# One encoder layer in fp32: the mixer as a pinned list schedule, and half of its gates stored in the place of x

## The chip, the cores and the metric

The kernel runs on one NeuronCore of a Trainium2 chip. The time is the device time of one execution in microseconds (us); the kernel before was timed three times. TensorE does the matmuls (PE, and PEld for its weight loads), VectorE (DVE) and ScalarE (ACT) the elementwise work, GpSimd (POOL) the decay tiles, SyncE (SP) issues the loads of weights.

## The reference, cut to what matters

One layer over 256 tokens of 1024 features, all in fp32: a half-step feed-forward network, a mixer of two branches, a second half-step network. The change touches the mixer alone.

```python
x = x + 1/2 * SwiGLU_1(RMSNorm(x))
h = RMSNorm(x);  u = h @ W_in
a = MLA(...)     # 16 heads: norms of q and k, rope, softmax(q k) v
m = BiSSD(...)   # 4 groups of 8 heads, conv of width 5 + SiLU, forward and backward scans
x = x + W_out( sigmoid(gA) * (a @ P_A) + sigmoid(gB) * (m @ P_B) )
x = x + 1/2 * SwiGLU_2(RMSNorm(x))
```

W_in holds, side by side, the latent columns of the attention, the columns of the SSD groups (z, x, B, C and the step sizes dt) and the two gates gA and gB. A scan over a chunk of 128 tokens is a product with a matrix of decays, exp(a[l] − a[s]), where a are cumulated logarithms:

```python
seg = a_cs[..., :, None] - a_cs[..., None, :]
decay = jnp.exp(jnp.where(tril, seg, -jnp.inf))
cb = jnp.einsum('bclgn,bcsgn->bcgls', cc, bc)
y_diag = jnp.einsum('bcgls,bcghls,bcsghp->bclghp', cb, decay, xdt)
```

## The kernel before

Weights and activations are each split into two reduced-precision pieces, hi and lo, and a product is the sum of three matmuls. `wload` (L131) loads 128x1024 weights (512 KB, SP's queue, tile raw), ACT copies them to whi (L113), DVE subtracts to get wlo (L116). `wstat` (L157) then issues three matmuls (L163, L164, L165) for each of 8 slices of 128 features: 24 matmuls for one piece, called a half below. Four buffers each hold raw, whi and wlo; four PSUM banks serve these products (ps_in, ps_half) and four (ps_g) all else. Activations stand in SBUF with features on partitions: x, and its scaled split xs.

The mixer runs in these steps.

- The first projection, three blocks into ps_in, gives the latent columns and dt. R is the norm row (L113, from ps_rows L230), by which DVE scales x into xr, split to xs (8 slices), and the first projection into cr, split to cqh, cql, ckh, ckl.
- The dt chain ends in ps_acs, the cumulated logarithms. ACT's queue writes them to DRAM as scr, from which the decay tiles are fetched.
- `in_group` (L562 on) makes ten halves for each SSD group: six with the convolution (ACT L582, then four DVE operations L119 on the tile xz), four plain ones for z, and one SiLU over all five xz tiles (L594).
- `ssd_group`: ps_cb (L709) is the matrix cb, ps_xT the transposed x. For each pair of heads POOL fetches a tile E of 128x768 from scr (L734) and adds the decays (L741, four operations per head), ACT takes Exp (L750), DVE multiplies by cb and sums (L116), PE makes ps_y (L760), DVE writes yg. A last step norms the group into ms. Six E buffers are shared by all heads.
- `attn_group`: eight groups of two heads, projection ps_qkv, transposes ps_qkT, scores ps_sc, softmax (L675), ps_pT, ps_o.
- `gates`: 16 halves through `half` (L792 on) into eight tiles gt; `branch0`: 8 halves of the SSD branch's output matrix for groups 0 and 1 into mpb. Sigmoids over gt follow (L837).
- The output: ps_ab (attention branch), ps_sb (second half of the SSD branch), the gated sum, and the last product ps_o, added to x.

The order of the steps is set by hand: `put` gives each step a number on a common line and `fill` spreads the halves of one group over one unit of it. All steps are written out in the order of these numbers, and a scheduler then orders each engine by its own rules, with the split of weights at a higher priority; the evictions of the last blocks (`paced`) hold back some Exps. The halves of group g+1 stand beside the scan of group g; the 16 gate halves stand beside the scan of group 3, after all blocks:

```python
        if g + 1 < G:
            xz, units = in_group(g + 1)
            if g == 2:
                units = units + [lambda c=c, j=j: branch0(c, j) for c in range(4) for j in range(2)]
        else:
            units = [lambda c=c, j=j: gates(c, j) for c in range(8) for j in range(2)]
        fill(g + F0, g + 1 + F0, units)
```

The functions that the change touches, with the line numbers of the profile:

Of the kernel before, what the change touches and what calls it, by code (L numbers as in the profile page):

```python
# [8 lines left out]
F32 = mybir.dt.float32  # L9
# [6 lines left out]
P = 128  # L16
# [21 lines left out]
PLC = ()  # L38
PLG = ()


A0 = -0.1293
DA = 0.2126
DB = 0.1251
S0 = 0.0991
DS = 0.1864
SF = 0.994

LA = 0.0317
LC = 0.0503  # L50
LF = 0.2546
HOLD = 0
AN = 1
F0 = 0.0148
F1 = -0.5421
# [7 lines left out]
G = 4  # L63
# [15 lines left out]
def _parts(value, bits, n):  # L79
    out = []  # L80
    rest = value
    for _ in range(n - 1):
        e = np.floor(np.log2(abs(rest)))
        q = 2.0 ** (e - bits + 1)
        part = np.floor(rest / q) * q
        out.append(float(part))
        rest -= part
    out.append(float(np.float32(rest)))
    return out


def build(ctx, tc, A, out, dbg=None):
# [87 lines left out]
    def rsqrt(y, v, n):  # L180
# [4 lines left out]
        ts(t, v.bitcast(I32), 1, None, ALU.logical_shift_right)  # L185
        ts(y.bitcast(I32), t, -1.0, float(0x5F3759DF), ALU.mult, ALU.add)
        ts(w, v, -0.5, None, ALU.mult)
        for _ in range(3):
            tt(a, y, y, ALU.mult)
            tt(a, a, w, ALU.mult)  # L190
            stt(y, a, 1.5, y, ALU.add, ALU.mult)
# [158 lines left out]
    scr = tc.dram_tile([32, 6, P], F32, name="scr")  # L350
    aneg = cp.tile([P, 64], F32, name="aneg")
# [69 lines left out]


    with ExitStack() as es:
# [30 lines left out]
        for k in range(KD):  # L454
            xr = m0.tile([P, T], F32, tag="xr", name="xr", bufs=2)
            stt(xr, x[:, k], vec[:, V_MIX + k:V_MIX + k + 1], R, ALU.mult, ALU.mult)
            split(xs[:, k, 0], xs[:, k, 1], xr)

        def latent(src, hi, lo, vcol, n):
            acc = sm.tile([P, T], F32, tag="nacc", name="lacc", bufs=1)  # L460
            for i, s in enumerate(src):
                if i == 0:
                    S.activation(acc, s, AF.Square)
                else:
                    sq = sm.tile([P, T], F32, tag="nsq", name="lsq", bufs=1)
                    S.activation(sq, s, AF.Square)
                    tt(acc, acc, sq, ALU.add)
                split(hi[:, i], lo[:, i], s, vec[:, vcol + i:vcol + i + 1])
            v = mp.tile([P, 2], F32, name=f"v_{vcol}", tag=f"v_{vcol}")
            ts(v, token_sums(ps_g, acc, "g"), 1.0 / n, EPS, ALU.mult, ALU.add)  # L470
            return v

        vq = latent(craw[0:3], cqh, cql, V_QA, 384.0)
        vk = latent(craw[3:5], ckh, ckl, V_KVA, 256.0)
        rk = mp.tile([P, 2], F32, name="rk")
        rsqrt(rk, vk, 2)
        hc = mp.tile([P, 2, 2], F32, name="hc")
        ts(hc[:, 0], vq, EPS * HD, None, ALU.mult)

        pt = gbank("ps_smt")  # L480
        for t in range(2):
            TE.transpose(pt[:, t * P:(t + 1) * P], craw[5][:, t * P:(t + 1) * P], ident)
        copy(smt, pt[:, :T].rearrange("p (a b) -> p a b", a=2))
        kpe = smt[:, :, 64:96]


        H = ROPE // 2
        kr = mp.tile([P, 2, ROPE], F32, name="kr")
        krs = m0.tile([P, 2, ROPE], F32, name="krs")
        kss = mp.tile([P, 2], F32, name="kss")  # L490
        tt(krs, kpe, kpe, ALU.mult)
        V.tensor_reduce(out=kss, in_=krs, axis=mybir.AxisListType.X, op=ALU.add)
        tt(kr, kpe, CCk, ALU.mult)
        tt(krs[:, :, 0:H], kpe[:, :, H:], SSk[:, :, 0:H], ALU.mult)
        tt(krs[:, :, H:], kpe[:, :, 0:H], SSk[:, :, H:], ALU.mult)
        tt(kr, kr, krs, ALU.add)
        ts(hc[:, 1], kss, EPS * HD, None, ALU.add)
# [3 lines left out]
        e = m0.tile([P, 2, 64], F32, name="dt_e")  # L501
        dt = m0.tile([P, 2, 64], F32, name="dt")
        tt(u, smt[:, :, 0:64], row[:, R_DTB:R_DTB + 64].unsqueeze(1).to_broadcast([P, 2, 64]), ALU.add)
        stt(e, u, -1.0, u, ALU.mult, ALU.max)
        S.activation(e, e, AF.Exp, scale=-1.0)
        S.activation(aneg, row[:, R_AL:R_AL + 64], AF.Exp)
        q = m0.tile([P, 2, 64], F32, name="dt_q")
        ts(q, e, 2.0, None, ALU.add)
        V.reciprocal(out=q, in_=q)
        tt(e, e, q, ALU.mult)  # L510
        tt(q, e, e, ALU.mult)
        pl = m0.tile([P, 2, 64], F32, name="dt_p")
        ts(pl, q, 1.0 / 17.0, None, ALU.mult)
        for c in (15.0, 13.0, 11.0, 9.0, 7.0, 5.0, 3.0):
            stt(pl, pl, 1.0 / c, q, ALU.add, ALU.mult)
        stt(pl, pl, 1.0, e, ALU.add, ALU.mult)
        ts(u, u, 0.0, None, ALU.max)
        stt(dt, pl, 2.0, u, ALU.mult, ALU.add)
        da = m0.tile([P, 2, 64], F32, name="da")
        stt(da, dt, -1.0, aneg.unsqueeze(1).to_broadcast([P, 2, 64]), ALU.mult, ALU.mult)  # L520
        dump("dt", dt)

        sgt = m0.tile([P, 2, P], F32, name="sgt")
        ts(sgt[:, 0], triF, 1.0, None, ALU.subtract)
        ts(sgt[:, 1], triB, 1.0, None, ALU.subtract)
        pa = gbank("ps_acs")
        for o, c, m in ((0, 0, sgt[:, 0]), (0, 1, triF), (32, 0, triB), (32, 1, sgt[:, 1])):
            TE.matmul(pa[:, c * 64 + o:c * 64 + o + 32], m, da[:, c, o:o + 32], start=True, stop=True)
        acs = m0.tile([P, 2, 64], F32, name="acs")
        V.tensor_copy(acs, pa[:, :P].rearrange("p (a b) -> p a b", a=2))  # L530
        nacs = mp.tile([P, 2, 64], F32, name="nacs")
        ts(nacs, acs, -1.0, None, ALU.mult)
        dup = m0.tile([P, 2, 2, 64], F32, name="dup")
        V.tensor_copy(dup, acs.unsqueeze(2).to_broadcast([P, 2, 2, 64]))
        pd = gbank("ps_dup")
        for c in range(2):
            TE.transpose(pd[:, c * P:(c + 1) * P], dup[:, c].rearrange("p a b -> p (a b)"), ident)
        acsT = m0.tile([P, T], F32, name="acsT")
        copy(acsT[0:64], pd[0:64, 0:T])
        for d in range(2):  # L540
            a = acsT[32 * d:32 * d + 32].rearrange("p (a b) -> p a b", a=2)
            o = 4 - 4 * d
            nc.scalar.dma_start(scr[:, o:o + 2], a)
            nc.scalar.dma_start(scr[:, 2 + d], a[:, 1 - d])

        lnd = mp.tile([P, 2, 64], F32, name="lnd")
        ts(u, dt, 2.0 ** -120, None, ALU.max)
        S.activation(lnd, u, AF.Ln)
        S.activation(e, lnd, AF.Exp, scale=-1.0)
        tt(e, e, u, ALU.mult)  # L550
        stt(lnd, e, -1.0, lnd, ALU.add, ALU.add)
        dump("acs", acs)
# [5 lines left out]
        m0_es.close()  # L558
        at_es = es.enter_context(ExitStack())
        at = at_es.enter_context(pool("attn", reuse_waits="tile"))  # L560

        paced = []

        def in_group(g):
            xz = [None] * 5
            cur = {}

            def half(c, j):  # L570
                if j == 0:
                    xz[c] = ss.tile([P, 2, T], F32, tag="xz", name="xz", bufs=10)
                    cur["ps"] = ps_mm.tile([P, 2, T], F32, tag="mm", name="ps_in1")
                xc, ps = xz[c], cur["ps"]
                (pc,) = wload(A["w_in1"][g, c, :, 1024 * j:1024 * j + 1024], [1024],
                              pool_lo=(0,) if 2 * c + j in PLC else ())
                wstat(ps[:, j], [(pc, 0, KD)], xs, 0, True, True)
                if c < 3:
                    i = 2 * c + j
                    ci = V_CW + (6 * g + i) * CW  # L580
                    cb = V_CB + 6 * g + i
                    last = S.activation(xc[:, j], ps[:, j], AF.Identity, bias=vec[:, cb:cb + 1],  # L582
                                        scale=vec[:, ci + 2:ci + 3])
                    for w in (0, 1, 3, 4):
                        s = w - 2
                        a0, a1 = max(0, -s), min(T, T - s)
                        stt(xc[:, j, a0:a1], ps[:, j, a0 + s:a1 + s], vec[:, ci + w:ci + w + 1],
                            xc[:, j, a0:a1], ALU.mult, ALU.add)
                elif j:
                    last = S.activation(xc, ps, AF.Copy)  # L590
                if c == 4 and j:
                    with tc.issue_after(last.ins), tc.high_priority():
                        for xc in xz:
                            last = S.activation(xc, xc, AF.Silu)  # L594
# [377 lines left out]
```

## Time and profile before

| | us |
|---|---|
| median of 3 runs | 808.74 |
| lowest and highest | 803.48, 808.98 |
| profiled execution | 806.14 |
| its span, first to last instruction | 804.2 |
| mixer, from R to the first ps_sb | 208.0 to 567.4 |
| first matmul of ps_cb, groups 0 to 3 | 271.4, 327.7, 403.9, 483.7 |
| gate halves on PE | 459.4 to 535.5 |
| decay tiles, first fetch to start of the last operation | 246.1 to 520.9 |

The page is made from one profiled execution. A row of instructions names line, engine, operation, output and inputs, shapes and count, then busy time and the mean of one in ns, then the idle time of the engine ahead of them and whose end released it. Matmuls are pipelined, so the mean of one is longer than the step from one to the next. The granted clock is the share of TensorE's full clock that was given.

### The profile page before, as it was taken

Reading aid. Unit: us, or ns where it says so; the run is one execution under the profiler, and the core shown is the slowest. Engines: PE = TensorE matmul, PEld = TensorE weight load, DVE = VectorE, ACT = ScalarE, POOL = GpSimd, SP = SyncE. Lnnn points to the kernel's source line nnn. Section 1 sums busy time; section 2 is a strip of 40 time slices with the busy share of each in tenths; the row PEclk is TensorE's granted clock in tenths of the full one; section 3 lists DMA queues with packets and bytes.
Section 4 is the critical chain, followed back from the end, with each engine's and each line's share of the span. In section 5 each row is a group of like instructions: output and inputs, shape, how many; then the busy total and the mean of one; then the engine's idle time right before and its main releaser. Section 6 shows DMA issues by size and latency. Waiting matters only on the chain.

```text
span 804.2 us, 13859 instructions
## 1 busy us (share of the span) xinstructions
PE 770.6 (96%) x5122; PEld 689.1 (86%) x5122; DVE 630.6 (78%) x1269; ACT 503.2 (63%) x887; POOL 169.1 (21%) x170
## 2 busy tenths in 40 slices
PE   7999999999989998899899989999999999999997
PEld 6888888888988887788888888898998888888886
DVE  5999887667788797899888877787787878877553
ACT  6666665555366787768679657767455666655441
POOL 0000000000004985855914482400000000000000
PEclk9999999999999999999999999999999999999999
DMA  7677764667117446247443744452655555554662
GB/s 270 198 229 236 224 230 142 182 189 221 51 57 232 152 163 226 76 146 243 125 146 122 241 150 138 143 184 88 210 174 185 182 185 188 188 194 129 204 206 72
DMA packets 43235, 139.10 MB, mean 173 GB/s; under 512 B 5152, under 2 KB 7200, under 8 KB 43168
## 3 DMA queue, kind: packets, MB, share of 16 engines
q1 hardware_dynamic: 40272, 125.43, 48.7%
q0 software_dynamic: 2560, 12.58, 4.9%
q8 instruction: 40, 0.66, 0.3%
q10 hardware_dynamic: 336, 0.20, 0.1%
q14 instruction: 27, 0.22, 0.1%
HBM read 137.05 MB, written 1.15 MB: 172 GB/s over the span
## 4 chain that ended last, share of the span: by engine, by line
PE 78%; DVE 13%; ACT 5%; issue 2%; DMA 1%; SPq 0%; DVEq 0%; ACTq 0%
PE ps_gu L176 20%; PE ps_d L176 10%; PE ps_gu L175 9%; PE ps_d L175 5%; DVE wlo L116 4%; PE ps_in L163 3%; PE ps_in L165 3%; PE ps_in L164 3%; PE ps_sc L666 2%; PE ps_y L760 2%; ACT whi L113 2%; PE ps_half L163 1%; PE ps_half L165 1%; PE ps_half L164 1%; DVE xz L119 1%
## 5 line engine op out<-in xcount | busy, mean ns | idle before, releaser
L113 ACT ACTIVATE whi<-raw 128x1024 fp32r<-128x1024 f32 (+4 forms) x260 | 250.9, 968 | 176.8 <-PE ps_d L176 51.5
L116 DVE TENSOR_TENSOR wlo<-raw,whi 128x1024 fp32r<-128x1024 f32 (+4 forms) x260 | 288.1, 1112 | 84.7 <-ACT whi L113 83.1
L176 PE MATMUL ps_gu<-xs,whi 128*128 128x512 f32 x704 | 243.0, 398 | 0.6 <-DVE xs L119 0.5
L175 PE MATMUL ps_gu<-xs,wlo 128*128 128x256 f32 x616 | 173.4, 281 | 3.6 <-DVE wlo L288 3.6
L741 POOL TENSOR_SCALAR E<-E,nacs 128x256 f32<-128x256 f32 (+1 forms) x128 | 148.8, 1178 | 25.7 <-DMA E<-scr 25.4
L176 PEld LDWEIGHTS ps_gu<-xs,whi 128*128 128x128 f32 x704 | 126.9, 189 | 25.3 <-DVE xs L119 1.2
L175 PEld LDWEIGHTS ps_gu<-xs,wlo 128*128 128x128 f32 x616 | 117.0, 190 | 8.3 <-DVE wlo L288 4.3
L176 PE MATMUL ps_d<-hs,whi 128*128 128x512 f32 x352 | 122.5, 393 | 0.0
L163 PE MATMUL ps_in<-xs,whi 128*128 128x256 f32 x368 | 109.1, 297 | 9.6 <-DVE xz L119 3.7
L165 PE MATMUL ps_in<-xs,wlo 128*128 128x256 f32 x368 | 107.4, 293 | 4.0 <-DVE wlo L116 4.0
L164 PE MATMUL ps_in<-xs,whi 128*128 128x256 f32 x368 | 107.1, 291 | 0.5 <-DVE xs L119 0.5
L175 PE MATMUL ps_d<-hs,wlo 128*128 128x256 f32 x336 | 94.7, 282 | 0.0
L734 POOL DMA_DIRECT2D E<-scr x32 | 18.0, 564 | 327.1 <-DVE wlo L116 245.7
L163 PEld LDWEIGHTS ps_in<-xs,whi 128*128 128x128 f32 x368 | 72.6, 198 | 13.4 <-ACT whi L113 5.0
L176 PEld LDWEIGHTS ps_d<-hs,whi 128*128 128x128 f32 x352 | 65.2, 188 | 13.8
L165 PEld LDWEIGHTS ps_in<-xs,wlo 128*128 128x128 f32 x368 | 72.5, 198 | 5.1 <-DVE wlo L116 4.6
L164 PEld LDWEIGHTS ps_in<-xs,whi 128*128 128x128 f32 x368 | 72.7, 198 | 1.7 <-issue 0.8
L175 PEld LDWEIGHTS ps_d<-hs,wlo 128*128 128x128 f32 x336 | 63.1, 188 | 0.7
L119 DVE SCALAR_TENSOR_TENSOR xz<-ps_in,vec,xz 128x254 f32<-128x254 f32 (+1 forms) x96 | 44.8, 477 | 6.0 <-ACT xz L582 5.5
L750 ACT ACTIVATE E<-E,lnd 128x256 f32<-128x256 f32 (+1 forms) x128 | 48.5, 450 | 0.0
L113 ACT ACTIVATE hs<-sg 128x256 fp32r<-128x256 f32 x44 | 18.1, 416 | 32.1 <-DVE sg L116 32.1
L163 PE MATMUL ps_half<-xs,whi 128*128 128x256 f32 x128 | 36.9, 289 | 0.0
(234 smaller groups left out, 1422.3 us busy)
## 6 DMA issues: line engine op xcount, KB each, us to landing
raw<-in_w_gu SPq DMA_DIRECT2D x86, 512.0 KB, 4.2
raw<-in_w_in SPq DMA_DIRECT2D x62, 512.0 KB, 4.7
raw<-in_w_d SPq DMA_DIRECT2D x32, 384.0 KB, 3.2
E<-scr POOLq DMA_DIRECT2D x32, 384.0 KB, 4.9
raw<-in_w_d SPq DMA_DIRECT2D x32, 320.0 KB, 3.4
raw<-in_w_sb SPq DMA_DIRECT2D x16, 512.0 KB, 4.2
raw<-in_w_ab SPq DMA_DIRECT2D x8, 512.0 KB, 3.8
raw<-in_w_o SPq DMA_DIRECT2D x8, 512.0 KB, 4.7
```

Source lines behind the costliest of these rows:

```text
L113: S.activation(dst, src, AF.Copy, scale=scale)
L116: V.tensor_tensor(out=dst, in0=a, in1=b, op=op)
L119: V.scalar_tensor_tensor(out=dst, in0=a, scalar=s, in1=b, op0=op0, op1=op1)
L163: TE.matmul(ps, pc.hi[:, w], xh, start=first and i == 0, stop=False)
L164: TE.matmul(ps, pc.hi[:, w], xl, start=False, stop=False)
L165: TE.matmul(ps, pc.lo[:, w], xh, start=False, stop=last and i == len(ks) - 1)
L175: TE.matmul(ps[:, 0], pc.lo[:, w], xs[:, k0 + i, 0], start=False, stop=False)
L176: TE.matmul(ps, pc.hi[:, w], xs[:, k0 + i], start=a, stop=b)
L666: TE.matmul(sc[:, t * T:(t + 1) * T], qk[:HD, t * P:(t + 1) * P], qk[:HD, T:2 * T], start=True, stop=True)
L734: nc.gpsimd.dma_start(E, scr[h].unsqueeze(0).to_broadcast([P, 6, P]))
L741: nc.gpsimd.tensor_scalar(out=E[:, a:a + n], in0=E[:, a:a + n], scalar1=nacs[:, c, w:w + 1], scalar2=0.0, op0=ALU.add, op1=ALU.min)
L750: ends[1] = S.activation(E[:, a:a + n], E[:, a:a + n], AF.Exp, bias=lnd[:, c, w:w + 1])
```

## The change

The mixer after the first projection is no longer written step by step. A class `Plan` collects steps, each of one engine (T, V, A, G for POOL, S for the loads): a cost from a small model (a fixed part and a part per element), a key, the steps on which it depends, and the rings of buffers from which it takes or to which it gives back. `Plan.run` then makes a list schedule: of each engine it takes the first step by key that can begin earliest, adds 1300 ns where ACT's function table changes, and adds a margin between engines. The steps are traced in that order, and each is pinned behind the step before it on its engine. Loads, splits, evictions, the operations of the norms and the parts of a scan are steps of their own; a half's 24 matmuls are three steps.

```diff
+class Plan:
+    FIX = {"V": 70, "A": 90, "G": 700}
+    PER = {"V": 1.04, "A": 0.83, "G": 2.4}
...
+    def run(self):
...
+            if s["table"] and s["table"] != table:
+                cost += 1300
+                table = s["table"]
...
+        for s in order:
+            bb = self.tc.nc.cur_bb.bb
+            n = len(bb.instructions)
+            with self.tc.issue_after(last[s["eng"]]) if s["eng"] in last else ExitStack():
+                s["fn"]()
+            last[s["eng"]] = bb.instructions[-1]
```

The keys count halves. Four gate halves are mixed among the ten of group 1 and four among the ten of group 2; the eight branch halves are mixed among those of group 3; the other eight gate halves come last. A group's scan begins when its SiLU is done, with one pair of heads for every 2.5 halves (3.5 in groups 2 and 3); attention group g has the key 8 + 6.5 g.

```diff
-A0 = -0.1293
-DA = 0.2126
...
+AK = 8.0
+AKD = 6.5
...
+SD = (2.5, 2.5, 3.5, 3.5)
...
+EA = 2
...
+NGT = (0, 4, 4, 0)
...
-        fill(g + F0, g + 1 + F0, units)
...
+            mix(ins[g], gts[o:n]) if g < G - 1 else mix(brs, ins[g], gts[o:n])
+            o = n
+        order += gts[o:]
```

The first eight gate halves are written into x itself, two of its eight feature tiles to each gate tile. x is spilled to DRAM by POOL's queue for that, twice (once after the first network, once as a step of the plan), and read back into four tiles xq, which the last product then uses.

```diff
+    spill = tc.dram_tile([P, KD, T], F32, name="spill")
...
+    nc.gpsimd.dma_start(spill, x)
...
+        spilled = do("G", 560, -30, lambda: nc.gpsimd.dma_start(spill, x), size=1 << 20)
...
-        gt = [None] * 8
+        gt = [x[:, 2 * c:2 * c + 2] for c in range(4)] + [None] * 4
...
+        for c in range(4):
+            xq.append(ss.tile([P, 2, T], F32, tag="xz", name="xq", bufs=10))
+            nc.gpsimd.dma_start(xq[c], spill[:, 2 * c:2 * c + 2])
...
-                tt(x[:, d], x[:, d], ps[:, j], ALU.add)
+                tt(x[:, d], xq[c][:, j], ps[:, j], ALU.add)
```

The fetch of a head now depends on the decays of the head two before it (EA = 2); the six small copies on POOL (L733, HOLD) are gone; the sigmoids depend on all scans, all attention groups and all gate halves.

```diff
-                    if g == 0 and p:
-                        nc.gpsimd.tensor_copy(E[:, 0, 0:1], xz[HOLD + p][:, 0, 0:1])
...
+                    d = do("G", 560, kh - LF, fetch, [rows_ready] + begun[-EA:][:1], take=["E"], size=393216)
```

Three places show what the order of the engines becomes. First DVE at the mixer's start, before: the four wlo of the first blocks of group 0 stand ahead of the norm (nv and rs_t are its first operations).

```order
L116 TENSOR_TENSOR wlo<-raw,whi 128x1024 x3
L119 SCALAR_TENSOR_TENSOR x<-ps_d,x 128x256
L123 TENSOR_SCALAR sgt<-cst 128x128
L119 SCALAR_TENSOR_TENSOR x<-ps_d,x 128x256
L123 TENSOR_SCALAR sgt<-cst 128x128
L116 TENSOR_TENSOR wlo<-raw,whi 128x1024
L119 SCALAR_TENSOR_TENSOR xs<-x,vec,xs 128x256
L116 TENSOR_TENSOR nacc<-nacc,nsq 128x256
L125 TENSOR_SCALAR nv<-ps_sum 128x2
```

The same engine after, where the first wlo of group 0 stands:

```order
L221 TENSOR_TENSOR cr<-ps_in_2225,R 128x512
L221 TENSOR_TENSOR xs<-xr,xs 128x256
L224 SCALAR_TENSOR_TENSOR cql<-cr,vec,cqh 128x256
L224 SCALAR_TENSOR_TENSOR ckl<-cr,vec,ckh 128x256
L230 TENSOR_SCALAR v_2306<-ps_sum 128x2
L224 SCALAR_TENSOR_TENSOR ckl<-cr,vec,ckh 128x256
L773 TENSOR_TENSOR wlo<-raw,whi 128x1024
L221 TENSOR_TENSOR dt_u<-smt,row 128x128
```

The first wlo moved from ahead of the norm to behind the third cr, all scaled slices and the splits of the latents.

Second ACT at the end of group 1's blocks, before: between the last plain eviction of xz and the SiLU nothing of the gates stands.

```order
L113 ACTIVATE whi<-raw 128x576
L675 ACTIVATE pr,sme<-ps_sc,mx,hr 128x256 x2
L113 ACTIVATE whi<-raw 128x512
L590 ACTIVATE xz<-ps_in_3452 128x512
L594 ACT_TABLE_LOAD
L594 ACTIVATE xz<-xz 128x512 x5
```

The same engine after, at the same place (x<-ps_half is the eviction of a gate half into x's place):

```order
L218 ACTIVATE whi<-raw 128x576
L1110 ACTIVATE ysq<-yg 128x512 x2
L218 ACTIVATE xs<-ps_o 128x256
L218 ACTIVATE whi<-raw 128x512
L218 ACTIVATE x<-ps_half 128x256
L218 ACTIVATE whi<-raw 128x1024
L218 ACTIVATE xz<-ps_in_3638 128x512
L1194 ACT_TABLE_LOAD
L1194 ACTIVATE xz<-xz 128x512 x5
```

A gate half, with its whi, its matmuls and its eviction, now stands among the blocks, four times in each of groups 1 and 2.

Third POOL in the last group's scan, before: fetches of one or two tiles at changing distances.

```order
L741 TENSOR_SCALAR E<-E,nacs 128x256
L734 DMA E<-scr 128x768
L741 TENSOR_SCALAR E<-E,nacs 128x256
L741 TENSOR_SCALAR E<-E,nacs 128x128 x2
L741 TENSOR_SCALAR E<-E,nacs 128x256
L734 DMA E<-scr 128x768 x2
```

The same engine after, one pair of heads and the fetches of the next:

```order
L1052 DMA E<-scr 128x768 x2
L1057 TENSOR_SCALAR E<-E,nacs 128x256
L1057 TENSOR_SCALAR E<-E,nacs 128x128 x2
L1057 TENSOR_SCALAR E<-E,nacs 128x256 x2
L1057 TENSOR_SCALAR E<-E,nacs 128x128 x2
L1057 TENSOR_SCALAR E<-E,nacs 128x256
L1052 DMA E<-scr 128x768 x2
```

Each pair's two fetches now stand directly ahead of the eight decay operations that use them, behind those of the pair before.

More of the change, by code (lines that the diff above doesn't have):

```diff
@@ L538, in build @@
[L538 to L549, printed above, removed]
@@ L556, in build @@
         mpb = mp.tile([P, 8, T], F32, name="mpb")
-        m0_es.close()
-        at_es = es.enter_context(ExitStack())
[L560 to L570, printed above, removed]
-                if j == 0:
-                    xz[c] = ss.tile([P, 2, T], F32, tag="xz", name="xz", bufs=10)
[L573 to L594, printed above, removed]
-                if c < 3 or j:
-                    paced.append(last)
-            return xz, [lambda c=c, j=j: half(c, j) for c in range(5) for j in range(2)]
```

848 lines of the change are left out of this document (581 added, 267 removed).

## The prediction

> **What bounds the kernel now.** I read the page first (busy times of the engines), then the mixer cut into stretches, then the waits inside them, last the single rows at its start. The page's first part:
>
> ```profile
> PE 770.6 (96%) x5122; PEld 689.1 (86%) x5122; DVE 630.6 (78%) x1269; ACT 503.2 (63%) x887; POOL 169.1 (21%) x170
> ```
>
> TensorE is busy 770.6 of 804.2 us, so less than 34 us can be won by order alone. The next view is the busy time by stretch: from the mixer's norm row R at 208 us to the first matmul of each SSD group (ps_cb at 271.4, 327.7, 403.9, 483.7) and on to the first ps_sb. Columns: the stretch, its length, PE, PEld, DVE, ACT and POOL busy with counts, granted clock, DMA share, GB/s. The last line is the first three stretches in one.
>
> ```profile
> core 0: us, PE busy (x) PEld busy (x) DVE busy (x) ACT busy (x) POOL busy (x), PEclk, DMA share, GB/s
> 208.00:271.40 63.40, 58.19 (x453) 55.90 (x454) 51.82 (x145) 41.22 (x75) 18.04 (x22) 0.97 0.40 127
> 271.40:327.70 56.30, 50.71 (x363) 43.85 (x362) 47.16 (x116) 41.25 (x86) 42.62 (x44) 0.97 0.50 165
> 327.70:403.90 76.20, 67.96 (x499) 62.08 (x498) 69.96 (x172) 57.00 (x116) 56.16 (x52) 0.96 0.46 147
> 403.90:483.70 79.80, 75.86 (x577) 67.85 (x575) 64.91 (x149) 57.50 (x118) 38.01 (x36) 1.00 0.52 169
> 483.70:567.40 83.70, 83.10 (x637) 74.46 (x637) 64.58 (x143) 58.98 (x121) 14.04 (x14) 1.00 0.45 143
> 208.00:403.90 195.90, 176.86 (x1311) 161.83 (x1312) 168.94 (x433) 139.47 (x274) 116.83 (x116) 0.97 0.45 146
> ```
>
> The mixer has two halves. In the head (to 403.9) PE is idle 195.90 − 176.86 = 19.0 us, and some of its busy time runs at a low clock. In the tail it is idle 3.9 + 0.6 = 4.5 us: there the count of matmuls sets the time. Who is late in the head? The busiest piece and its waits (us in total, times, longest):
>
> ```profile
> 310.00:390.00 80.00, 67.92 (x475) 60.17 (x472) 67.41 (x172) 55.15 (x111) 57.62 (x57) 0.94 0.52 167
> PE ps_in L165 <- DVE wlo L116: 3.0, 2, 1.6
> PE ps_in L163 <- DVE xz L119: 2.9, 2, 1.8
> PE ps_in L163 <- ACT whi L113: 2.5, 2, 1.7
> PE ps_in L163 <- DVE hr L119: 2.0, 1, 2.0
> ```
>
> DVE is named in three of the four (7.9 of 10.4 us), yet with shares from 82% to 92% it is not full either: it waits for ACT and PE in turn. The head is a knot of queues in a loose order, with DVE the nearest to being a bound. The low clock, in four places:
>
> ```profile
> 262.00:267.00 5.00, 4.85 (x25) 4.21 (x24) 2.08 (x5) 2.30 (x4) 3.37 (x9) 0.66 0.61 205
> 316.00:321.00 5.00, 3.40 (x17) 3.25 (x16) 3.75 (x9) 2.49 (x5) 4.62 (x6) 0.66 0.45 154
> 340.00:345.00 5.00, 4.43 (x24) 4.42 (x24) 5.00 (x15) 3.39 (x8) 0.97 (x1) 0.66 0.17 46
> 385.00:390.00 5.00, 4.70 (x26) 4.70 (x27) 4.17 (x12) 0.15 (x1) 5.00 (x5) 0.66 0.81 228
> ```
>
> Each loses 0.34 × 5.00 = 1.7 us, 6.8 in all. So the most that the head can give back is 19.0 + 6.8 = 25.8 us.
>
> **The change, part by part.**
>
> *Gates moved.* Before, all 16 gate halves follow the last in-projection block; now eight stand in the head, between the blocks of groups 1 and 2. One half is one 512 KB load on SP's queue, whi and its eviction on ACT, wlo on DVE and 24 matmuls. Prices, from 30 us of full PE and from the groups of 250 to 572 us (count, busy, mean ns):
>
> ```profile
> 570.00:600.00 30.00, 30.00 (x254) 29.87 (x253) 24.02 (x40) 14.32 (x21) 0.00 (x0) 1.00 0.55 178
> L116 DVE TENSOR_TENSOR wlo<-raw,whi 128x1024 fp32r<-128x1024 f32 (+2 forms) x81 | 91.8, 1141 | 12.7 <-ACT whi L113 12.3
> L113 ACT ACTIVATE whi<-raw 128x1024 fp32r<-128x1024 f32 (+2 forms) x81 | 79.5, 988 | 45.5 <-PE ps_in L164 18.1 <-PE ps_half L164 11.5 <-PE ps_ab L164 8.5
> L797 ACT ACTIVATE gt<-ps_half 128x256 f32<-128x256 f32 x16 | 6.0, 372 | 0.0
> ```
>
> A matmul takes 30.00/254 = 0.118 us, a half 24 × 0.118 = 2.83. The tail loses 8 × 2.83 = **−22.7 us** in full, since PE is its bound.
>
> What the head pays is the open term. Bounds: if PE is always fed at full clock, the head takes 176.86 − 6.8 + 22.7 = 192.8 us, 3.1 less than now, though it does more. If DVE keeps its share, 168.94/195.90 = 0.862, the head takes (168.94 + 8 × 1.141)/0.862 = 178.1/0.862 = 206.6, 10.7 more. The list schedule pins every engine to an order that its model found without long waits, so I expect better than 0.862; the best that the trace shows over a whole stretch is 69.96/76.20 = 0.918. I take the middle, 0.89: 178.1/0.89 = 200.1, **+4.2 us**. ACT rises by 8 × (0.988 + 0.372) = 10.9 to 150.4 us and DMA by 4 MB on 146 GB/s at a share of 0.45; neither comes near 200 us, so both cost nothing while that holds.
>
> *The start.* Before, four weight pieces of group 0 were ready ahead of R; now the first whi stands on ACT behind the last xs and ckh, and the first wlo on DVE behind the third cr and ckl. The rows (start, duration, what), then the busy times there:
>
> ```profile
> 199.51 1.22 DVE L116 TENSOR_TENSOR wlo<-raw,whi 128x1024 fp32r<-128x1024 f32 x1
> 207.84 0.70 PE L230 MATMUL ps_rows<-diag,ones 128*128 128x256 f32 x2 [0.20 <-DVE diag L123]
> 217.76 0.69 DVE L116 TENSOR_TENSOR cr<-ps_in,R 128x512 f32<-128x512 f32 x1
> 218.87 0.50 ACT L113 ACTIVATE ckh<-cr,vec 128x256 fp32r<-128x256 f32 x1
> 208.00:217.00 9.00, 9.00 (x74) 8.95 (x75) 7.90 (x20) 5.71 (x15) 0.00 (x0) 1.00 0.01 2
> 217.00:222.00 5.00, 5.00 (x43) 4.82 (x42) 4.11 (x20) 2.52 (x6) 0.00 (x0) 1.00 0.00 0
> 222.00:235.00 13.00, 12.66 (x104) 12.28 (x103) 12.87 (x44) 7.97 (x12) 0.00 (x0) 1.00 0.27 78
> 235.00:245.00 10.00, 7.66 (x60) 7.03 (x60) 7.35 (x19) 5.58 (x9) 0.00 (x0) 1.00 0.35 101
> ```
>
> After ps_rows 74 matmuls of the first projection are left, so PE runs dry at about 217. The first pair of pieces is there at 218.87 + 0.50 + 0.99 + 1.14 = 221.5. Two short sums in between take perhaps half a microsecond: PE stands for about 4 us where it now works 5.00 of 5.00. Behind it on PE stand all blocks and, through ps_acs and the scr rows, POOL's first fetch. Ends: 2 (part of the 2.34 us idle of 235 to 245 is filled by the work pushed back) to 6 (4 and a clock drop of 1.7). I take **+4**.
>
> The clock: in the trace it fell right after a half-idle piece.
>
> ```profile
> 312.00:316.00 4.00, 1.97 (x11) 1.25 (x9) 1.77 (x5) 3.59 (x7) 4.00 (x4) 1.00 1.00 352
> 316.00:320.00 4.00, 2.40 (x12) 2.25 (x11) 3.75 (x9) 2.49 (x5) 4.00 (x5) 0.69 0.48 157
> ```
>
> PE worked 1.97 of 4.00 us at clock 1.00, and then had 0.69. [...]
>
> *POOL and the decay tiles.* Before, fetches (L734) run ahead of the decays (L741) in varying depth, up to four at a time; now each pair issues two fetches only after the decays of the pair before, so every landing stands between. Rows:
>
> ```profile
> L734 POOL DMA_DIRECT2D E<-scr x32: 538/538/724, 246.1 to 508.8; - x32
> DMA to landing us min/median/max: 3.4/4.9/7.2
> L734 POOL DMA_DIRECT2D E<-scr x32 | 18.0, 564 | 327.1 <-DVE wlo L116 245.7 <-PE ps_y L760 33.2 <-DVE yg L119 19.8
> L760 PE MATMUL ps_y<-E,xt x128: 379/379/431, 282.7 to 545.6; 128*64 128x256 f32 x128
> L741 POOL TENSOR_SCALAR E<-E,nacs 128x256 f32<-128x256 f32 x64 | 84.8, 1330 | 25.7 <-DMA E<-scr 25.4
> L741 POOL TENSOR_SCALAR E<-E,nacs 128x128 f32<-128x128 f32 x64 | 65.1, 1025 | 0.0
> ```
>
> A pair costs POOL 2 × 0.56 + 4.9 + 4 × (1.330 + 1.025) = 15.4 us. Sixteen pairs take 247 us from the first fetch at 246.1 to 493, ahead of the last ps_y at 545.6. So POOL hides under the rest; only the last group, whose blocks and gates no longer cover it so long, can wait. There the last pair goes fetch, landing, decays (15.4) and then Exp, product and ps_y on three engines, for which I allow 3.5: 19 us, against some 154 matmuls, 154 × 0.118 = 18.2 us, between the group's start and the next long PE run. That is 0 to 3 us; I take **+1**, nearer the lower end because PE's heavier fp32 matmuls (0.38 us) stretch the cover.
>
> *The rest.* Two spills of x (1 MB each, POOL's queue) go out at 206 to 222, where DMA moves 0 to 2 GB/s; gates that write x come tens of microseconds later. Four read-backs stand behind POOL's last decay and are first needed after ps_sb, which runs for over 20 us: hidden, unless POOL is late itself. The six HOLD copies vanish from POOL, which was idle there. The sigmoids keep their number. I put all at 0.
>
> Sum: −22.7 + 4.2 + 4 + 1 = −13.5. The profiled execution took 806.1 us (span 804.2 and 1.9 around it), below the median of 808.74 by 2.6; 806.1 − 13.5 = 792.6, so **793**.
>
> **Rivals.**
>
> *The knot dissolves.* The head takes its PE bound (−3.1), the start +2, the tail nothing more: −23.8, so 782. For it: 67.96 of 76.20 is PE's poorest long stretch, and only order keeps it so. Against it: DVE would run at 178.1/192.8 = 92% over the whole head, which it does only in the best stretch.
>
> *DVE keeps its share.* +10.7 in the head, start +6, tail +3: −22.7 + 19.7 = −3.0, so 803. For it: three of the four waits name it. Against: the waits are 1 to 2 us each, behind pieces that the new order puts further ahead of their matmuls.
>
> *Slower: POOL's pair becomes the bound.* From the first fetch (246.1 + 4 = 250) to where the last ps_y would be (545.6 − 13 = 532) are 282 us, 17.6 per pair, against 15.4. Every microsecond over 17.6 costs 16. How much slower does POOL get where DVE is fuller? Two windows, 300 to 330 and 330 to 395 us:
>
> ```profile
> L741 POOL TENSOR_SCALAR E<-E,nacs 128x256 f32<-128x256 f32 x9 | 10.9, 1212 | 0.1
> L741 POOL TENSOR_SCALAR E<-E,nacs 128x256 f32<-128x256 f32 x18 | 25.9, 1447 | 3.7 <-DMA E<-scr 3.6
> L741 POOL TENSOR_SCALAR E<-E,nacs 128x128 f32<-128x128 f32 x16 | 17.2, 1084 | 0.0
> ```
>
> The large operation goes from 1212 to 1447 ns. With the 1447 and 1084 of the second window and the longest landing, 7.2, a pair takes 1.1 + 7.2 + 4 × (1.447 + 1.084) = 18.4 us: 16 × 0.8 = 13, and the gain is gone. That is the point from which it decides. Fetches also wait for ps_y, which frees their tiles, 33.2 us now; half of that again in the pinned row is 1 us a pair, 19.4: 16 × 1.8 = +29, so 822. Against it: with the median landing the slower pair is at 16.1, under 17.6, and a wait for ps_y adds only where PE is late as well. [...]
>
> **How the numbers follow.** Chances: my forecast (786 to 798) 0.50; the knot dissolves, about 782, 0.14; DVE keeps its share, about 803, 0.21; POOL's pair as the bound, 815 and above (822 by the sum), 0.15. Within 1% of 806.1, about what a measurement of this kernel can tell from no change, is 798 to 814. Faster is then 0.50 + 0.14 = 0.64, same 0.21, slower 0.15. The range runs from 781 (the first rival with half of its start hidden in idle time that is there anyway) to 806, DVE's case with another 3: it leaves out the slower case and a little of the first.
>
> **What would show it.** The head, from R to the third SSD start, with eight gate halves among it, should take about 204 us with the start's stall; the tail from there to ps_sb about 23 less than 163.5. The start should show 4 us of idle PE ahead of the first ps_in of group 0, ended by wlo. POOL should show one wait for its DMA in each pair, some 75 us in all, with no ps_y late by more than 3. I am wrong if PE's idle time in the tail rises above 8 us, if POOL's pair period passes 17.6, or if DVE's share of the head stays at 0.86 with PE waiting for wlo and xz as before.

## The result and the profile after

| | before | after |
|---|---|---|
| median, us | 806.45 (4 runs, 803.48 to 808.98) | 785.35 (4 runs, 783.85 to 787.65) |
| profiled execution, us | 806.14 | 786.83 |
| its span, us | 804.2 | 785.1 |
| mixer, ps_rows of R to the first ps_sb, us | 207.8 to 567.4 = 359.6 | 206.8 to 548.0 = 341.2 |

The ratio is 0.9742, with a 95% interval of 0.969 to 0.9795: 2.6% faster, 21.1 us by the medians and 19.3 us between the two profiled executions. 18.4 of these 19.3 us lie in the mixer. First the page's busy times of the changed kernel:

```profile
PE 759.7 (97%) x5122; PEld 684.6 (87%) x5122; DVE 632.1 (81%) x1269; ACT 497.4 (63%) x887; POOL 179.7 (23%) x170
```

The matmuls are the same 5122. PE's idle time fell from 33.6 to 25.4 us, and its busy time from 770.6 to 759.7. Of the fall in busy time about 2.6 us go with the granted clock (0.988 before, 0.991 after: 0.012 × 804.2 − 0.009 × 785.1, an estimate). The rest isn't accounted for; the rows of matmuls overlap (at 214 us of the changed kernel one lasts 0.28 us and the next starts 0.12 us after it), so busy time may hold short pauses too. The stretches of the mixer, cut at the starts of the four groups' ps_cb as in the prediction (length, busy times of PE, PEld, DVE, ACT, POOL, clock, DMA share, GB/s); the last two rows are head (first three) and tail (last two):

```profile
core 0: us, PE busy (x) PEld busy (x) DVE busy (x) ACT busy (x) POOL busy (x), PEclk, DMA share, GB/s
206.80:269.60 62.80, 57.14 (x438) 55.50 (x439) 53.86 (x139) 41.78 (x75) 18.97 (x17) 0.95 0.46 151
269.60:347.70 78.10, 73.35 (x565) 67.13 (x564) 72.21 (x171) 59.22 (x121) 48.95 (x48) 0.98 0.56 181
347.70:410.20 62.50, 61.33 (x478) 55.62 (x477) 59.83 (x150) 49.27 (x106) 37.83 (x33) 1.00 0.50 164
410.20:494.30 84.10, 81.25 (x642) 74.51 (x641) 76.70 (x195) 64.18 (x138) 54.38 (x52) 1.00 0.54 175
494.30:548.00 53.70, 52.99 (x409) 47.60 (x408) 40.75 (x75) 40.26 (x80) 18.13 (x18) 1.00 0.49 162
206.80:410.20 203.40, 191.82 (x1475) 178.25 (x1476) 185.90 (x458) 150.26 (x300) 105.75 (x96) 0.97 0.51 167
410.20:548.00 137.80, 134.23 (x1048) 122.11 (x1047) 117.44 (x270) 104.44 (x217) 72.51 (x69) 1.00 0.52 170
```

Two sums matter here. The head holds 164 matmuls more than the 1311 of before and takes 203.4 us instead of 195.9: 7.5 us for work of 164 × 0.118 = 19.4. The tail holds 165 fewer than 1213 and takes 137.8 instead of 163.5, 25.7 us less. PE's idle time in the head fell from 19.0 to 11.6 us, that of the tail from 4.5 to 3.6.

The two sums hold more than the gates. Counted by tile, the head gained the 192 matmuls of the gates and 98 of the attention, and 126 matmuls of the blocks left it for the tail. In the tail, two of these groups before (first two rows) and after (last two):

```profile
L163 PE MATMUL ps_in<-xs,whi 128*128 128x256 f32 x24 | 6.9, 286 | 0.0
L616 PE MATMUL ps_qkv<-whi,cqh 128*128 128x192 f32 x24 | 6.7, 281 | 0.0
L268 PE MATMUL ps_in<-xs,whi 128*128 128x256 f32 x66 | 19.8, 299 | 2.1 <-DVE xz L224 1.1 <-DVE rs_w L228 1.0
L854 PE MATMUL ps_qkv<-whi,cqh 128*128 128x192 f32 x12 | 3.2, 268 | 0.0
```

### The profile page after: what moved, and what is told of

It reads as the page before. It is cut to its first block, busy times and chain, and to the rows that moved or that the text cites. A ratio compares the mean times of both kernels' runs of the same rounds, so it can differ in the third digit from the quotient of the medians.

```text
span 785.1 us, 13906 instructions
## 1 busy us (share of the span) xinstructions
PE 759.7 (97%) x5122; PEld 684.6 (87%) x5122; DVE 632.1 (81%) x1269; ACT 497.4 (63%) x887; POOL 179.7 (23%) x170
## 4 chain that ended last, share of the span: by engine, by line
PE 74%; DVE 18%; ACT 3%; issue 2%; DMA 2%; SPq 0%; ACTq 0%; DVEq 0%
PE ps_gu L281 21%; PE ps_d L281 10%; PE ps_gu L280 9%; PE ps_d L280 5%; DVE wlo L773 5%; DVE xz L224 4%; PE ps_in L268 3%; PE ps_in L270 3%; PE ps_in L269 2%; DVE E L221 2%; PE ps_half L268 2%; PE ps_half L269 1%; PE ps_half L270 1%; PE ps_y L1088 1%; PE ps_gu L283 1%
## 5 line engine op out<-in xcount | busy, mean ns | idle before, releaser
L221 DVE TENSOR_TENSOR wlo<-raw,whi 128x1024 fp32r<-128x1024 f32 (+2 forms) x180 | 198.4, 1104 | 72.5 <-ACT whi L218 71.7
L1057 POOL TENSOR_SCALAR E<-E,nacs 128x256 f32<-128x256 f32 (+1 forms) x128 | 158.5, 1254 | 58.7 <-DMA E<-scr 54.2
L773 DVE TENSOR_TENSOR wlo<-raw,whi 128x1024 fp32r<-128x1024 f32 (+2 forms) x80 | 89.5, 1133 | 12.6 <-ACT whi L218 12.6
L1063 ACT ACTIVATE E<-E,lnd 128x256 f32<-128x256 f32 (+1 forms) x128 | 47.6, 457 | 0.0
```

What stands on the lines that cost most here:

```text
L221: V.tensor_tensor(out=dst, in0=a, in1=b, op=op)
L773: (V if low_on == "V" else nc.gpsimd).tensor_tensor(out=pc.lo[:, :s_], in0=pc.raw[:, :s_], in1=pc.hi[:, :s_], op=ALU.subtract)
L1057: nc.gpsimd.tensor_scalar(out=E[:, a:a + n], in0=E[:, a:a + n], scalar1=nacs[:, c, w:w + 1], scalar2=0.0, op0=ALU.add, op1=ALU.min)
L1063: S.activation(E[:, a:a + n], E[:, a:a + n], AF.Exp, bias=lnd[:, c, w:w + 1])
```

## The experiments

Each experiment ran beside the kernel before on the same chip; that one's median was 807.8, 808.9 and 808.1 us in the three groups of four, so a ratio is given with each time.

**1. The gates behind the blocks again, plan and pins kept.**

```diff
-NGT = (0, 4, 4, 0)
+NGT = (0, 0, 0, 0)
```

> The changed kernel with all 16 gate halves behind the blocks again (NGT = (0, 0, 0, 0)), planned and pinned as before. If the gates were what filled PE's pauses in the head: the tail gets 8 x 2.83 = 22.7 us back; the head (203.4 us, DVE busy 185.9 = 91%) keeps its DVE share, so it shrinks only to (185.9 - 8 x 1.13)/0.914 = 193.5 us, 9.9 less: 785.4 + 12.8 = 798 us. Rival, the new order alone took the pauses out: PE is fed with or without gates, head and tail exchange 22.7 us, and the time stays within 2 us of 785.

Measured: 806.97 us, ratio 1.0 (0.9973 to 1.0028). All of the gain is gone; the planned order alone wins nothing. It cost 9 us more than the filling theory said, and the profile shows where. Its stretch between 366 and 405 us, and then the same span of time in the changed kernel:

```profile
366.00:405.00 39.00, 24.79 (x110) 16.55 (x111) 31.47 (x89) 24.07 (x59) 30.20 (x33) 0.65 0.28 89
```

```profile
366.00:405.00 39.00, 38.10 (x303) 34.71 (x302) 37.45 (x102) 28.21 (x56) 24.69 (x23) 1.00 0.55 180
```

With the gates last, PE does 110 matmuls there instead of 303 and is idle 14.2 us, and the clock is granted at 0.65. That is 0.35 × 39 = 13.7 us of clock, but not as much lost time, since PE waits for other engines in the same stretch. What stands ahead of PE there (POOL's time line of the first experiment from group 1's last pair on, the branch halves on PE, and the busy times from the end of the last ps_y on):

```profile
352.32 15.06 POOL L1057 TENSOR_SCALAR E<-E,nacs 128x256 f32<-128x256 f32 x8 [2.94 <-DMA E<-scr]
371.15 7.38 POOL L1057 TENSOR_SCALAR E<-E,nacs 128x256 f32<-128x256 f32 x8 [2.69 <-DMA E<-scr]
378.49 1.16 POOL L1052 DMA_DIRECT2D E<-scr  x2
382.76 9.05 POOL L1057 TENSOR_SCALAR E<-E,nacs 128x256 f32<-128x256 f32 x8 [3.10 <-DMA E<-scr]
391.76 1.12 POOL L1052 DMA_DIRECT2D E<-scr  x2
395.88 9.10 POOL L1057 TENSOR_SCALAR E<-E,nacs 128x256 f32<-128x256 f32 x8 [3.00 <-DMA E<-scr]
L268 PE MATMUL ps_half<-ms,whi x64: 274/282/775, 401.5 to 471.7; 128*128 128x256 f32 x64
376.60:397.30 20.70, 11.97 (x68) 7.51 (x65) 20.35 (x70) 12.50 (x30) 14.59 (x15) 0.75 0.33 104
386.04 2.35 DVE L773 TENSOR_TENSOR wlo<-raw,whi 128x1024 fp32r<-128x1024 f32 x2
```

POOL goes from pair to pair, with no rest but the landings of about 3 us. The eighth pair, the last of group 1's scan, leaves POOL at 367.4, the last ps_y of that group starts at 377.2, and the group's norm is done for the first branch half only at 401.5. In these last 24 us POOL is no longer what the norm waits for. For the most part DVE is: it is busy 20.35 of 20.70 us, and the small operations of the norm stand in its row among two wlo of later blocks, eight operations of the convolution and the products of the next scan (last two rows). So the stall has two parts, POOL's pace up to 367 us and DVE's full row behind it. The blocks of group 3 can't go ahead: their xz tiles need the buffers of group 1's scan, and in the pinned order they stand behind the first branch halves. So PE has only short pieces of attention and of the next scan left, and no blocks, gates or branch halves. In the changed kernel 22.7 us of gates are in front of that place.

**2. The gates moved, in the kernel before with its order by hand.**

```diff
+                else:
+                    n = len(units)
+                    mixed = [((i + 0.5) / n, 0, u_) for i, u_ in enumerate(units)]
+                    mixed += [((i + 0.5) / 4, 1, lambda c=2 * g + i // 2, j=i % 2: gates(c, j)) for i in range(4)]
+                    units = [u_ for _, _, u_ in sorted(mixed, key=lambda z: z[:2])]
             else:
-                units = [lambda c=c, j=j: gates(c, j) for c in range(8) for j in range(2)]
+                units = [lambda c=c, j=j: gates(c, j) for c in range(4, 8) for j in range(2)]
```

> The kernel before, its order by hand and its free scheduler kept, with only the gates moved: four halves mixed into group 1's blocks, four into group 2's, stored in the place of x, x spilled once and read back. If the move is the gain: about as much as the forecast's own sum for it, 806.5 - 22.7 + 4 to 10 = 788 to 794 us. Rival, the planned order is the gain and the knot in the head stays: DVE at its 86% takes 10.7 us more in the head, POOL and the hand-set distances are upset: 794 to 806 us.

Measured: 834.69 us, ratio 1.0371 (1.0348 to 1.0394), beyond what either theory allowed. The last two stretches of this kernel, and PE's two longest waits in the last one:

```profile
409.10:499.70 90.60, 82.82 (x646) 75.85 (x645) 71.35 (x162) 66.28 (x143) 50.16 (x49) 1.00 0.51 162
499.70:595.00 95.30, 74.94 (x446) 56.55 (x445) 54.88 (x134) 45.75 (x88) 11.29 (x15) 0.82 0.29 92
PE ps_pT L685 <- DVE pr L123: 10.3, 4, 3.0
PE ps_qkT L663 <- DVE ka L116: 2.9, 2, 2.7
```

The final stretch holds 446 matmuls instead of 637 and takes longer than before (95.3 against 83.7): attention heads and the last scan stand there with too little beside them, and PE idles 20.4 us, 13.2 of it for softmax and keys. The clock at 0.82 is up to 0.18 × 95.3 = 17 us more, as far as it doesn't fall into the idle time. So neither part of the change is worth anything alone, the move at least not in this order by hand: the plan without the move is 1 us from the kernel before, the move without the plan 27 us slower.

**3. The plan without its pins.**

```diff
-            with self.tc.issue_after(last[s["eng"]]) if s["eng"] in last else ExitStack():
+            with ExitStack():
```

> The changed kernel with its steps traced in the planned order, but without the pins that hold each engine to it. If the pinned order of each engine is what counts: 4 us or more slower, 790 to 797. Rival, the traced order is enough and the scheduler keeps it closely: within 2 us of 785.

Measured: 804.11 us, ratio 0.9963 (0.9933 to 0.9993). Nearly all of the gain hangs on the pins. In the groups of the mixer the loads of ACT's function table stand out (line, engine, operation, count, busy, mean ns); first the kernel without pins, then the changed one:

```profile
L1194 ACT ACT_TABLE_LOAD x11 | 14.1, 1283 | 0.2
L1063 ACT ACT_TABLE_LOAD x10 | 12.8, 1283 | 5.7 <-DMA E<-scr 5.6
L1208 ACT ACT_TABLE_LOAD x6 | 7.7, 1283 | 0.1
L958 ACT ACT_TABLE_LOAD x4 | 5.1, 1283 | 5.5 <-DVE mx L224 5.5
```

```profile
L1063 ACT ACT_TABLE_LOAD x3 | 3.8, 1283 | 0.1
L1194 ACT ACT_TABLE_LOAD x3 | 3.8, 1283 | 0.1
L958 ACT ACT_TABLE_LOAD x1 | 1.3, 1283 | 0.0
L1208 ACT ACT_TABLE_LOAD x1 | 1.3, 1283 | 0.0
```

The scheduler mixes SiLU (L1194) and sigmoid (L1208) with Exp (L1063, L958): the groups of the mixer have 31 table loads here instead of 8, each an instruction of 1.283 us on ACT. In the changed kernel no more than 0.1 us of idle time stands ahead of the loads of these groups.

**4. The first weight pieces ahead of the norm.**

```diff
+        early = [wload(A["w_in1"][0, n // 2, :, 1024 * (n % 2):1024 * (n % 2) + 1024], [1024])[0] for n in range(4)]
...
-            (pc,), e = load(key, src, [1024], low_on="G" if key in PLO else "V")
+            (pc,), e = ([early.pop(0)], []) if early else load(key, src, [1024], low_on="G" if key in PLO else "V")
```

> The changed kernel with the first four weight pieces of group 0 loaded and split ahead of the norm, as in the kernel before. If the start's stall (1.8 us idle between 217 and 222) and the two half-clock stretches after it (3.4 us lost) are on the path: about 5 us faster, 780. Rival: what is won is given back, because those four splits stand in DVE's way at the end of the first network (ps_rows was 1.0 us later in the kernel before) and the time saved is idled away at ps_acs (2.3 us there before): 0 to 2 us, 783 to 786.

Measured: 780.73 us, ratio 0.9699 (0.9679 to 0.9719); the changed kernel's ratio is 0.9742. The first stretch of this kernel:

```profile
207.60:263.60 56.00, 54.16 (x449) 53.58 (x450) 49.69 (x135) 37.17 (x67) 11.59 (x12) 1.00 0.47 151
```

It takes 56.0 us instead of 62.8, at clock 1.00 instead of 0.95, with 11 matmuls more; 0.8 us are given back before it, where ps_rows starts at 207.6 instead of 206.8. The time falls by 4.6 us by the medians and by 3.5 by the two ratios, whose intervals overlap; the runs themselves (780.00 to 781.77 against 783.85 to 787.65) don't. The start's stall was on the path.

**5. The first eight gate halves among group 3's blocks.**

```diff
-NGT = (0, 4, 4, 0)
+NGT = (0, 0, 0, 8)
```

> The changed kernel with the first eight gate halves mixed into group 3's blocks instead of groups 1 and 2 (NGT = (0, 0, 0, 8)). With the gates last, PE stood from about 366 to 402 us ahead of the first branch half, which needs the norm of group 1's scan, whose decay tiles POOL delivers at 13.8 us a pair. If the gates help by covering POOL up to that point, they come too late here, since the first of them stand behind a branch half: 797 to 808 us. Rival, it is enough that gates stand anywhere ahead of the last blocks: 783 to 789 us.

Measured: 808.37 us, ratio 0.9986 (0.9947 to 1.0025). The gates still stand ahead of the last blocks, but behind the first branch half (second row), and there they are worth nothing. It is the place that counts.

```profile
L268 PE MATMUL ps_half<-xs,whi x128: 277/283/471, 412.1 to 542.9; 128*128 128x256 f32 x128
L268 PE MATMUL ps_half<-ms,whi x64: 274/282/561, 405.3 to 505.2; 128*128 128x256 f32 x64
```

**6. Pins on ACT alone.**

```diff
-            with self.tc.issue_after(last[s["eng"]]) if s["eng"] in last else ExitStack():
+            with self.tc.issue_after(last[s["eng"]]) if s["eng"] in last and s["eng"] == "A" else ExitStack():
```

> The changed kernel with the pins on ScalarE alone, the other engines left to the scheduler. Without any pins ACT loaded its function table 40 times instead of 15, 25 x 1.283 = 32 us of ACT, and the time was 804. If the pins matter by the grouping of tables: 784 to 789 us. Rival, the pins on PE and DVE matter as much: 792 to 804 us.

Measured: 787.52 us, ratio 0.9726 (0.9661 to 0.979), the same as with all pins within the noise. The tables are loaded as often as in the changed kernel (15 times in all). So ACT's pinned order is enough for what the pins are worth; pins on all engines but ACT weren't tried, and whether ACT's order helps by the tables alone isn't separated from its other effects. The orders of PE, DVE and POOL come out well enough by themselves when the steps are written in the planned order.

**7. The second experiment with its attention drawn ahead.**

```diff
-DA = 0.2126
-DB = 0.1251
+DA = 0.17
+DB = 0.105
```

> The second experiment's kernel (order by hand, gates moved) with the attention heads drawn ahead (DA from 0.2126 to 0.17, DB from 0.1251 to 0.105), so that the last head stands at key 3.1 instead of 3.8. There the tail took 95.3 us with PE idle 20.4 and the clock at 0.82, waiting for softmax and keys. If the gates had been the cover of the attention's chains in the tail: 20 to 30 us faster than the 834.7, 805 to 815. Rival, the heads ahead only overload the busier head part: 825 or more.

Measured: 833.97 us, ratio 1.0294 (1.0208 to 1.038). A miss for the theory behind it. In the profiled execution (841.31 us, the longest of the four) the fourth stretch now has the loss (429.5 to 555.9 us, PE busy 113.91 of 126.4, clock 0.93): the wait moved with the heads. Why the order by hand bears the move so badly isn't settled.

**8. Gates last, fetches of decay tiles four heads ahead.**

```diff
-EA = 2
+EA = 4
...
-NGT = (0, 4, 4, 0)
+NGT = (0, 0, 0, 0)
```

> The first experiment's kernel (gates last, planned and pinned) with fetches of decay tiles free to run four heads ahead of the decays (EA = 4 instead of 2), so that POOL need not wait about 3 us for a landing in each pair. If POOL's chain up to the first branch half is what costs the 21.6 us there: 8 pairs x 3 us earlier, up to 24 us of stall and the clock drop go, 788 to 797 us. Rival, the stall has another cause (the attention's or the norm's chain, or simply too few matmuls): 803 to 808 us.

Measured: 800.01 us, ratio 0.9878 (0.9811 to 0.9945), 7 us better than the first experiment by the medians and 3.7 between the two profiled executions, and 3 us short of the expected range. POOL is done with group 1's last pair at 361.3 instead of 367.4 us: 6.1 us for 8 pairs, not 24: up to 370 us it waits 21.0 us for landings instead of 26.8, and 8.2 instead of 0.9 for a ps_y that frees a tile. The gain is of the size of these 6 us, so POOL's pace is a part of that stall. But the first branch half starts at 399.8, only 1.7 us earlier (3.8 counted from R, which is 2.1 later here): the rest is the group's norm in DVE's row, which is busy 27.38 of the 30 us from 370 to 400.

**9. Blocks as cover instead of gates.** The place of x holds four xz tiles of group 3, and four halves of that group come ahead of the first branch half:

```diff
+        def place(g, c):
+            return x[:, 2 * c:2 * c + 2] if in_x(g, c) else ss.tile([P, 2, T], F32, tag="xz", name="xz", bufs=10)
...
-            mix(ins[g], gts[o:n]) if g < G - 1 else mix(brs, ins[g], gts[o:n])
+            mix(ins[g], gts[o:n]) if g < G - 1 else (mix(ins[g][:4]), mix(brs, ins[g][4:]))
```

> Gates last as in the first experiment, but the place of x holds four of the five xz tiles of group 3 instead of eight gate halves, and four halves of group 3's blocks stand ahead of the first branch half; the ten xz buffers otherwise keep group 3 waiting for group 1's scan. If what the gates give is cover, matmuls that wait for no scan, then four such halves are worth 4 x 2.83 = 11 us and part of the clock loss: 790 to 798 us. Rival, the gates matter in another way (the shorter tail itself, or their ACT and DVE work): 803 to 808 us.

Measured: 799.01 us, ratio 0.9888 (0.985 to 0.9926): 8 us better than the first experiment, 1 us short of the range. Matmuls of another kind in the same place help too, by about 8 of the 21.6 us between the first experiment and the changed kernel. Four halves seem too few for the whole: the stretch after the third ps_cb (376.4 to 474.1 us) still has the clock at 0.88.

**10. The changed kernel with fetches ahead.**

```diff
-EA = 2
+EA = 4
```

> The changed kernel with fetches of decay tiles four heads ahead (EA = 4), nothing else. There POOL waited 54.2 us for landings. If these lie off the path, as the prediction costed them in the head: 783.5 to 787 us. Rival, POOL's pace sets the scans and through them the blocks that wait for xz buffers: 3 us or more faster, below 782.

Measured: 788.33 us, ratio 0.975 (0.9712 to 0.9787): no gain, and perhaps a loss too small to tell. POOL's waits for landings fall from 54.2 to 35.6 us, and nothing comes of it. POOL itself ends no earlier (its last decay operation starts at 523.6 us, at 520.7 in the changed kernel), since other waits take the place. So the landings are off the path with the gates in place; what a faster POOL would bring wasn't tried.

**11. The fourth experiment with fetches ahead and one spill.**

```diff
-    nc.gpsimd.dma_start(spill, x)
...
-EA = 2
+EA = 4
```

> The fourth experiment's kernel (pieces of group 0 ahead of the norm, 780.7 us) with fetches four heads ahead and the first of the two spills of x left out. If POOL and the spill are off the path: 779.5 to 782. Rival, POOL's waits are on it once the start is gone: 775 to 778.

Measured: 781.51 us, ratio 0.9673 (0.9641 to 0.9704), within the spread of the fourth. The fourth experiment is the fastest by its median, this one by its ratio; the two can't be told apart.

**12. Less work for DVE in the head.**

```diff
-                d = do(low_on, [s_], key - WL, low, [d], give=["raw"])
+                if low_too:
+                    d = do(low_on, [s_], key - WL, low, [d], give=["raw"])
```

> The changed kernel without the subtraction that makes wlo for the eight gate halves in the head; their third matmul reads whi, so the gates come out less exact and PE's work is the same. DVE's work in the head falls by 8 x 1.13 = 9.1 us of 185.9. If DVE's share (91% there) bounds the head, as in the prediction's sum: 9.1/0.914 = 10 us less, 775 to 778. Rival, the head is bound by PE and by chains through the scan, and DVE is merely busy: 783 to 787.

Measured: 786.14 us, ratio 0.9727 (0.9683 to 0.977). The head of this kernel:

```profile
205.70:407.50 201.80, 191.54 (x1474) 177.90 (x1475) 177.42 (x446) 150.73 (x300) 102.71 (x99) 0.97 0.51 170
```

DVE is busy 177.42 us instead of 185.90, and the head takes 201.8 instead of 203.4; the whole is no faster, and DVE's share falls to 88%. Its share does not set the head's length. DVE isn't off the path for that: in the chain of work that ended last, wlo is 15.4% of the changed kernel's head and 7.2% of this one's, and PE's blocks took up what it left.

## Why the prediction was right, and where its steps were not

The direction was right, and 785.35 lies in the range of 781 to 806. It is 0.65 us below the forecast's own span of 786 to 798, nearer in number to the rival that the knot dissolves (782), though that rival had the head 3.1 us shorter, and it came out 7.5 longer.

**The tail, −22.7 and +1 for POOL.** Measured −25.7, with 165 matmuls fewer rather than 192: the 192 of the gates and 99 of the attention left the tail, and 126 of group 3's blocks came into it, which the sum didn't have. Right in kind; the size is another sum. Gates and blocks together are 66 fewer, 66 × 0.118 = 7.8 us, and PE's idle time fell by 1.0; the other 16.9 us, 0.17 for each attention matmul if all is put on these (an estimate), aren't resolved further. The last group's chain through POOL cost nothing that shows: PE is idle 0.71 of 53.70 us in the last stretch.

**The head, +4.2, and the start, +4: together +8.2.** Measured +7.5. The sum comes out, in part by luck: one of its two steps is wrong, and the work in the head is not the work that it had. "The middle, 0.89" of DVE's share was to set the head's length, with DVE busy 178.1 us. DVE was busy 185.9 us at a share of 91%, with attention work in the head that the sum didn't have, and experiment 12 took 8.5 us from it and won nothing. The share is a result of a head that goes faster, not its bound. What the head runs against is closer to PE with a few short waits: 191.8 of 203.4 us busy, with 1.8 us of the idle time and 3.4 of lost clock in the start.

**The start.** PE idled as forecast, in rows of the changed kernel from its windows between 217 and 228 us, cut where the clock changes, and from its time line:

```profile
217.50:220.90 3.40, 1.59 (x10) 1.15 (x11) 3.37 (x10) 3.38 (x7) 0.00 (x0) 1.00 0.03 5
220.90:224.30 3.40, 3.40 (x18) 3.40 (x17) 3.33 (x13) 3.39 (x5) 0.00 (x0) 0.50 0.53 178
224.30:227.70 3.40, 3.40 (x18) 3.40 (x18) 3.03 (x11) 0.01 (x1) 0.00 (x0) 0.50 0.36 130
218.87 0.39 PE L268 MATMUL ps_in<-xs,whi 128*128 128x256 f32 x1 [1.05 <-ACT whi L218]
220.13 0.39 PE L270 MATMUL ps_in<-xs,wlo 128*128 128x256 f32 x1 [0.76 <-DVE wlo L773]
```

The wait itself was 1.8 us, under half of the 4 expected: PE began on whi at 218.87, before wlo was there at 220.13, which the sum hadn't allowed for, and the two short sums ahead of it filled about 1 us instead of half of one. The clock made up for it: 6.8 us at 0.50, 3.4 lost instead of the 1.7 allowed for at the upper end. Together 5.2, between the ends of 2 and 6, so the +4 was near by two errors that offset each other. Experiment 4 got 3.5 to 4.6 back.

**POOL.** A wait for the landing in each pair was forecast at some 75 us; the page has 54.2 in 15 waits. They are hidden, as experiment 10 shows. From the first fetch (243.3) to the end of the last decays (522.7) the sixteen pairs took 17.5 us each, close under the 17.6 from which POOL was to decide; much of that is POOL waiting for others, as for a ps_y that frees a tile (19.9 us). The rival that POOL's pace becomes the bound is a true mechanism of this kernel, but of the one without the move: in experiments 1 and 5 the scan of group 1 and its norm (in experiment 1 in DVE's row) stand in the way of all blocks that PE has left.

**The spills and the read-back at 0.** The trace agrees. The spills were issued at 199.0 and 204.3 us, somewhat earlier than forecast, and a gate first writes into x at 270.1; the read-backs were issued by 524.3 and are first needed at 578.8, and the longest of these transfers took 6.1 us to land. Experiment 11 leaves one spill out and shows no gain, but it changes the fetches as well.

**What the prediction didn't see.** It took the move of the gates to cost the head and pay the tail, with the better order as a help. The experiments show that the parts don't add: the move alone loses 27 us, the plan alone gains nothing, both gain 21. The gates pay because they wait for no scan and stand at the one place where the plan would otherwise run dry of long runs of matmuls. And the gain needs ACT's order, for whose table loads the sum has no term: without any pins the time is 804, with ACT's alone 787.5. The 23 more table loads in the groups of the mixer (23 × 1.283 = 29.5 us of ACT) are the plainest difference; that they are the whole cause is argued, not shown.

## What to carry to other kernels

Matmuls that depend on nothing late are a reserve; look for the place where PE's planned order has only work behind one long chain (with the gates last, 110 matmuls instead of 303 in the 39 us from 366 to 405), and put the reserve just ahead of it, not at the end where it is easy to hold. A norm of a few small operations took 24 us in the first experiment, where it stood in a row that was busy 20.35 of 20.70 us. Before calling the busiest engine the bound, take a known piece of its work away: 8.5 us taken from an engine at 91% won nothing here. Where one engine pays for changes of mode (here 1.283 us for each table load, 31 loads without pins against 8), pin that engine's order first; here it gave as much as the pins on all of them (787.5 against 785.35 us, within the noise).

## What the runs showed of the hardware

In the changed kernel a stall of PE cost more in clock than in time. A window of 3.4 us with PE busy 1.59 us, at clock 1.00, was followed by 6.8 us at clock 0.50, though PE was busy all through them (rows above): 3.4 us lost for 1.8 us of waiting. From 227.7 to 229.4 us the clock was at 0.99 again.

POOL's large operation (128x256) took 1.524 us on average in the changed kernel and 1.330 before, with DVE busy 81% of the span instead of 78%; the small one (128x128) 0.984 and 1.025. The slowing that the prediction feared came, at 15% of the one and none of the other. That DVE is its cause isn't shown: over both sizes the mean is 1.287 us in the first experiment at a DVE share of 79%, and 1.254 in the changed kernel at 81%. The means hide a wide spread; a single decay operation took 0.70 to 3.14 us in the changed kernel and up to 6.40 in the first experiment. The changed kernel's rows:

```profile
L1057 POOL TENSOR_SCALAR E<-E,nacs 128x256 f32<-128x256 f32 x64 | 97.2, 1524 | 58.7 <-DMA E<-scr 54.2 <-DVE xz L224 4.5
L1057 POOL TENSOR_SCALAR E<-E,nacs 128x128 f32<-128x128 f32 x64 | 62.4, 984 | 0.0
```
